# Attention units of four query blocks, with a unit's transpositions between the next unit's scores

## The chip, the cores and the metric

The kernel runs on one core of a Trainium2 chip. A core has engines that each run their own instructions in order and wait for one another by semaphores: TensorE (PE; its weight loads are shown as PEld), VectorE (DVE), ScalarE (ACT), GpSimd (POOL) and SyncE (SP), which issues the DMA transfers here. Matmuls write to PSUM; everything else lives in SBUF. The metric is the device time of one execution, in microseconds (us), as the median of several runs.

## The reference

A two-layer decoder trunk on one sequence of 1024 tokens of width 1024. Each layer projects the stream once and feeds four token mixers of four heads each (64 columns of values a head): MLA, stick-breaking attention, forgetting ("Fox") attention and cross-attention to a memory of 256 tokens. Three of them are causal: a block of 128 queries reads the keys up to its own end.

```python
def _layer(x, mem, cos, sin, w_in, ...):
    h = x @ w_in
    ...
    y_mla = _causal_softmax_attention(concat([q_nope, q_pe]), concat([k_nope, k_pe]), v_mla)
    y_sb = _stick_breaking_attention(sq, sk, sv)
    y_fox = _causal_softmax_attention(fq, fk, fv, log_decay=c)
    y_mem = _memory_attention(mem_q, mk, mv)
    ...
    for n in range(N_BRANCHES):
        yb = branches[n].reshape(b, s, BRANCH_WIDTH) * jax.nn.silu(gate_z[:, :, n])
        merged = merged + merge_g[:, :, n] * (yb @ w_branch[n])
    out = merged @ w_out
    return _layer_norm(DEEPNORM_ALPHA * x + out, ln_g, ln_b)
```

In a causal softmax mixer a query block does `logits = q k^T (+ decay)`, a row maximum, `exp`, a sum, and `p v`; stick-breaking has a suffix product over the keys of `1 - sigmoid` in place of the softmax. All is float32. The kernel writes most operands as a sum of two parts, a leading one (`h`) and the rest (`l`), and multiplies the parts apart.

## The kernel before

**Projections.** The projections keep 128 columns of weights on PE and move 512 tokens at a time: for each of eight contraction blocks three matmuls, `h h`, `l h`, `h l` (`passes`, L255 to L257). They are written as generators that stop after each such step, so that they can be handed out between the pieces of attention work: the *filler*.

**Units.** Attention is cut into units (`Unit`, L367): one head and one group `qg` of two query blocks, 256 queries. A unit has two parts:

- `scores` (L388): for each of its query blocks and each 512 keys a score tile `sc` in PSUM (two matmuls, L383 and L384, and a third for MLA, L386; the second uses `s2`, a copy of the queries with their two halves exchanged, which `swapped`, L360, makes with two DMAs). Fox and MLA: DVE adds bias or mask and takes the maximum (L441), ACT does `exp` (L135), DVE the reciprocal (L452), POOL the scaling (L453). Stick-breaking: ACT makes two sigmoids `kt` and `bt` of each tile (L135), DVE a scan (L446) and a product (L447).
- `values` (L463): PE transposes the probabilities by blocks of 128 x 128 (L472) into a PSUM tile `pt`: two key blocks x two query blocks, 512 columns, 384 on the diagonal. ACT copies it to `ph` (L155), DVE writes the rest `pl` (L156). `product` (L495), two `pt` later (`LAG`), multiplies: for each key block `y += v ph` and `y += v pl`, 256 columns each, 128 where the diagonal leaves one query block (L502). At a unit's end `add_heads` adds the two halves of `y` with ACT (`yc`, L490) and DVE (L491).

**Order.** `run` (L540) takes a list of units, writes a unit's scores, and then the values of the unit that lies two back (`AHEAD`). At each stop `gap` hands out so many steps of filler that `total` steps are spread evenly over all gaps of the run. The groups of a head come in the order 3, 0, 2, 1. A layer has six such runs: two Fox pairs (49 filler steps each), two stick-breaking pairs (65 and 64), memory (72) and MLA (54 steps of the merge between them, then `finish`). In the merge (`merge`, L1080) the gated branch outputs are split by `split_y` (ACT `ybh`, L158; DVE `ybl`, L159) from `y`, which `load_y` (L1062) reads back from a DRAM buffer `y_d`. The program is then put in order for each engine by a list scheduler of the framework, by its own durations; so the rows of an engine are not simply those of the text.

**Buffers that tie engines together.** PSUM: score tiles and projections share four buffers (`pj`, `sc`) that are handed out in the program's order; `pt` (and the transpositions `vtp` of a new pair's values, L336) has two, `y` has two.

## Time and profile before

| | |
|---|---|
| time, median of 3 runs | 1570.71 us (1570.52 to 1572.05) |
| the profiled execution | 1573.47 us, its span 1571.7 us |
| granted TensorE clock | 0.999 |
| PE matmuls of attention values (L502) | 1088: 896 of 256 columns, 192 of 128 |
| transpositions (L472) | 992, in 272 evacuations |

A row of the page's fifth part has line, engine, operation, `out<-in` with shapes and count, then busy time and the mean ns of one, then the idle time of that engine just before those rows and what ended it. A row of the timeline has start, duration, engine, line and operation, and in square brackets how long the engine had stood before it and for what. Matmuls overlap in the array, so the distance from one start to the next is what one costs, not the duration printed.

### The profile page before, as it was taken

Reading aid. Unit: us, or ns where it says so; the run is one execution under the profiler, and the core shown is the slowest. Engines: PE = TensorE matmul, PEld = TensorE weight load, DVE = VectorE, ACT = ScalarE, POOL = GpSimd, SP = SyncE. Lnnn points to the kernel's source line nnn. Section 1 sums busy time; section 2 is a strip of 40 time slices with the busy share of each in tenths; the row PEclk is TensorE's granted clock in tenths of the full one; section 3 lists DMA queues with packets and bytes.
Section 4 is the critical chain, followed back from the end, with each engine's and each line's share of the span. In section 5 each row is a group of like instructions: output and inputs, shape, how many; then the busy total and the mean of one; then the engine's idle time right before and its main releaser. Section 6 shows DMA issues by size and latency. Waiting matters only on the chain.

```text
span 1571.7 us, 24749 instructions
## 1 busy us (share of the span) xinstructions
PE 1552.4 (99%) x8446; PEld 1326.9 (84%) x8446; DVE 1034.5 (66%) x2055; ACT 726.9 (46%) x1608; POOL 781.1 (50%) x951
## 2 busy tenths in 40 slices
PE   9999999999999999999999999999999999999997
PEld 8888888888888788888898888888888888888886
DVE  7455687755436788882853566887554367898738
ACT  4355565545434666440323556655354346564400
POOL 5666536565544343671336655365565443436600
PEclk9999999999999999999999999999999999999999
DMA  6321112132233211252313211121322232212413
GB/s 185 113 73 42 46 47 70 58 100 76 76 107 110 68 45 55 80 175 74 124 55 106 60 47 48 42 75 51 108 70 80 102 111 71 65 41 78 154 53 115
DMA packets 86061, 127.92 MB, mean 81 GB/s; under 512 B 13424, under 2 KB 38832, under 8 KB 85936
## 3 DMA queue, kind: packets, MB, share of 16 engines
q1 hardware_dynamic: 85936, 126.34, 25.9%
q8 instruction: 67, 1.10, 0.3%
q14 instruction: 58, 0.48, 0.1%
HBM read 89.57 MB, written 19.96 MB: 70 GB/s over the span
## 4 chain that ended last, share of the span: by engine, by line
PE 92%; DVE 2%; POOL 2%; issue 2%; DMA 1%; ACT 1%; SPq 0%; DVEq 0%; POOLq 0%; ACTq 0%
PE pj L255 13%; PE pj L257 13%; PE pj L256 13%; PE y L502 7%; PE pt L472 6%; PE po L256 4%; PE po L257 4%; PE po L255 4%; PE sc L384 4%; PE sc L383 4%; PE pb L255 3%; PE pb L257 3%; PE pb L256 3%; PE pg L255 1%; PE pg L257 1%
## 5 line engine op out<-in xcount | busy, mean ns | idle before, releaser
L255 PE MATMUL pj<-xTh,wh 128*128 128x512 f32 x832 | 334.3, 402 | 2.3 <-DVE mx L441 1.4
L257 PE MATMUL pj<-xTh,wl 128*128 128x512 f32 x832 | 327.4, 393 | 0.0
L256 PE MATMUL pj<-xTl,wh 128*128 128x512 f32 x832 | 326.2, 392 | 0.0
L164 POOL TENSOR_SCALAR wh<-wr 128x512 fp32r<-128x512 f32 x168 | 114.9, 685 | 227.6 <-PE pj L256 147.1
L167 POOL TENSOR_TENSOR wl<-wr,wh 128x512 fp32r<-128x512 f32 x168 | 223.2, 1331 | 9.7
L156 DVE TENSOR_TENSOR pl<-pt,ph 128x384 fp32r<-128x384 f32 (+1 forms) x272 | 171.3, 639 | 85.0 <-ACT ph L155 83.2
L155 ACT CAST ph<-pt 128x384 fp32r<-128x384 f32 (+1 forms) x272 | 147.5, 549 | 151.3 <-PE pt L472 147.3
L257 PEld LDWEIGHTS pj<-xTh,wl 128*128 128x128 f32 x832 | 156.3, 188 | 31.6
L255 PEld LDWEIGHTS pj<-xTh,wh 128*128 128x128 f32 x832 | 156.7, 188 | 24.9 <-DVE mx L441 1.8
L256 PEld LDWEIGHTS pj<-xTl,wh 128*128 128x128 f32 x832 | 156.7, 188 | 22.5
L453 POOL TENSOR_SCALAR p<-p,sm 128x896 f32<-128x896 f32 (+7 forms) x128 | 102.7, 804 | 146.7 <-DVE sm L452 146.2
L135 ACT ACTIVATE p<-p,mx 128x896 f32<-128x896 f32 (+7 forms) x128 | 99.5, 777 | 68.0 <-DVE mx L441 61.0
L502 PE MATMUL y<-pl,v 128*128 128x256 f32 (+1 forms) x544 | 121.9, 301 | 0.0
L135 ACT ACTIVATE mg<-pg 128x512 f32<-128x512 f32 x128 | 76.1, 598 | 84.0 <-PE pg L257 43.1
L502 PE MATMUL y<-ph,v 128*128 128x256 f32 (+1 forms) x544 | 112.5, 282 | 2.1 <-ACT ph L155 1.9
L472 PE MATMUL pt<-ident_r,p 128*128 128x128 f32 x704 | 111.2, 273 | 0.3
L502 PEld LDWEIGHTS y<-ph,v 128*128 128x128 f32 x544 | 94.9, 189 | 16.3 <-ACT ph L155 2.1
L446 DVE TENSOR_TENSOR_SCAN kt<-kt,unseen 128x896 f32<-128x896 f32 (+3 forms) x64 | 95.2, 1490 | 19.8 <-ACT kt L135 19.3
L255 PE MATMUL pb<-ybh,wh 128*128 128x512 f32 x256 | 102.5, 400 | 1.5 <-ACT mg L135 0.7
L256 PE MATMUL pb<-ybl,wh 128*128 128x512 f32 x256 | 100.1, 391 | 0.0
L257 PE MATMUL pb<-ybh,wl 128*128 128x512 f32 x256 | 100.1, 391 | 0.0
L472 PEld LDWEIGHTS pt<-ident_r,p 128*128 128x128 f32 x704 | 85.1, 140 | 13.8 <-issue 0.5
(272 smaller groups left out, 3550.8 us busy)
## 6 DMA issues: line engine op xcount, KB each, us to landing
wr<-in_w_s_dram SPq DMA_DIRECT2D x168, 256.0 KB, 2.6
s<-opA SPq DMA_DIRECT2D x128, 64.0 KB, 2.0
s<-opB SPq DMA_DIRECT2D x128, 64.0 KB, 2.0
wr<-in_w_out_dram SPq DMA_DIRECT2D x32, 256.0 KB, 2.6
xr<-in_x_t_dram SPq DMA_DIRECT2D x16, 256.0 KB, 5.3
ckb<-c_d SPq DMA_DIRECT2D x8, 512.0 KB, 3.8
y_d<-y SPq DMA_DIRECT2D x16, 256.0 KB, 2.1
y<-y_d SPq DMA_DIRECT2D x16, 256.0 KB, 3.4
```

Source lines behind the costliest of these rows:

```text
L135: i = act.activation(*args, **kw)
L155: act.copy(h, src)
L156: return dve.tensor_tensor(l, src, f(h), ALU.subtract)
L164: i = pool.tensor_scalar(h, src, 1.0, 1.0, ALU.mult, ALU.mult)
L167: pool.tensor_tensor(l, src, f(h), ALU.subtract)
L255: pe.matmul(ps, ah, bh, start=k == 0, stop=False)
L256: pe.matmul(ps, ah, bl, start=False, stop=False)
L257: pe.matmul(ps, al, bh, start=False, stop=k == nk - 1)
L446: dve.tensor_tensor_scan(kt[:, ::-1], kt[:, ::-1], unseen[:, S - w:][:, ::-1], 1.0, ALU.mult, ALU.max)
L453: pool.tensor_scalar(p, p, sm, 1.0, ALU.mult, ALU.mult)
L472: pe.transpose(pt[:, c:c + P], self.p[i][:, b * P:(b + 1) * P], ident)
L502: pe.matmul(u.y[:, q0 * P:256], u.op["v"][b][:, u.head, :], src[:, s * 256 + q0 * P:s * 256 + 256], start=j == 0 and n == 0, stop=j == n_c ...
```

## The change

A unit now has one head and one *half*: four query blocks, 512 queries, in the order 1, 0. Four effects follow.

1. `chunks` gives one key block at a time, with the first query block `q0` that may see it: a `pt` holds one key block x four query blocks, 512 columns, and 384, 256 and 128 on the diagonal. `product` has two matmuls for it, `v ph` and `v pl`. Value matmuls, each with its weight load, fall from 1088 to 640; the columns that they move stay the same. The evacuations of `pt` rise from 272 to 320, some of them now 256 and 128 wide.
2. `s2` is 512 wide, with half as many DMAs of twice the size. `add_heads` works on 512 columns, half as often.
3. `run` no longer keeps two units in flight. While it writes a unit's scores, it takes the steps of the one unit before it between them, from the second score tile on, spread evenly; what is left comes behind the scores.
4. In the MLA run 100 - 26 - 16 steps are spread instead of 96 - 26 - 16; `finish` sets `prep[0]` behind the last product, so that the gates `pg` of the merge then use the buffers of `y`; and the first merge calls `split_y` for the next branch at its end, each half two stops later, instead of within its last column block.

```diff
-    def swapped(q, head, qg):
-        s2 = tp.tile([P, 256], F32R, tag="s2", name=nm("s2"), bufs=3)
-        src = q[head][qg // 2][:, (qg % 2) * 256:(qg % 2) * 256 + 256]
+    def swapped(q, head, half):
+        s2 = U("s2")
+        src = q[head][half]
...
-            for i in range(2):
-                qb = 2 * self.qg + i
+            for i in range(4):
+                qb = 4 * self.half + i
...
-            g = self.qg
-            return [[(2 * j, 0, 0), (2 * j + 1, 1, 0)] for j in range(g)] + [[(2 * g, 1, 0), (2 * g + 1, 0, 1)]]
+                return [(0, 0), (1, 0)]
+            return [(b, max(0, b - 4 * self.half)) for b in range(4 * self.half + 4)]
...
-                for b, s, q0 in ch:
-                    for i in range(q0, 2):
-                        c = s * 256 + i * P
-                        lo = min(lo, c)
-                        pe.transpose(pt[:, c:c + P], self.p[i][:, b * P:(b + 1) * P], ident)
+                for i in range(q0, 4):
+                    pe.transpose(pt[:, i * P:(i + 1) * P], self.p[i][:, b * P:(b + 1) * P], ident)
...
-        seq = [(b, s, q0, ph) for b, s, q0 in ch] + [(b, s, q0, pl) for b, s, q0 in reversed(ch)]
-        for n, (b, s, q0, src) in enumerate(seq):
-            pe.matmul(u.y[:, q0 * P:256], u.op["v"][b][:, u.head, :], src[:, s * 256 + q0 * P:s * 256 + 256],
-                      start=j == 0 and n == 0, stop=j == n_ch - 1 and n == len(seq) - 1)
+        for n, src in enumerate((ph, pl)):
+            pe.matmul(u.y[:, q0 * P:], u.op["v"][b][:, u.head, :], src[:, q0 * P:],
+                      start=j == 0 and n == 0, stop=j == n_ch - 1 and n == 1)
...
-            for _ in u.scores():
+            back = flight.pop(0) if flight else None
+            vals = back.values() if back else iter(())
+            n_vals = 2 * len(back.chunks()) if back else 0
+            told = 0
+            for n, _ in enumerate(u.scores(), 1):
+                gap()
+
+                while told * (u.n_scores - 1) < n_vals * max(0, n - 2):
+                    told += 1
+                    if next(vals, 0) == 0:
+                        break
+                    gap()
+            for _ in vals:
                 gap()
             flight.append(u)
-            if len(flight) > AHEAD:
-                for _ in flight.pop(0).values():
-                    gap()
...
-                    if ct == KT - 1 and following is not None:
+                    if ct == KT - 1 and following is not None and not first:
                         split_y(following, half)
...
+            if first:
+
+                for half in range(2):
+                    yield
+                    yield
+                    split_y(following, half)
...
-        run(units(ml[0], "mla") + units(ml[1], "mla"), mg, 96 - MG_EARLY - MG_LATE, False)
-        finish(mg, 1)
+        run(units(ml[0], "mla") + units(ml[1], "mla"), mg, 100 - MG_EARLY - MG_LATE, False)
+        finish(mg, 1, lambda: prep.__setitem__(0, True))
```

The mem units get two score tiles in the same way. Lines move by a few: the value matmuls are L495, the transpositions L467, `ph` and `pl` L153 and L154, the projections L253 to L255, the scores L382 and L383, the `v` copies L338 and L340, `add_heads` L484 and L485.

How the rows of an engine stand is shown at three places. The names are those of the tiles, with a number that tells one buffer's use from another.

The first place is the end of the first Fox pair and the start of the second (some 122 us into the program): PE's rows in the kernel before, where `pj` is the second pair's projection, `vtp` the transposition of its values, `sc` its first scores, and `pt` and `y` belong to the first pair's last units.

```order
L257 MATMUL pj_1634<-xTh_179,wl_1449 128x512
L336 MATMUL vtp_1589<-ident_r,vT_1576 128x128 x4
L383 MATMUL sc_1649<-opA_1321,opA_1182 128x512
L384 MATMUL sc_1649<-opA_1321,s_335_1600 128x512
L383 MATMUL sc_1656<-opA_1440,opA_1182 128x512
L384 MATMUL sc_1656<-opA_1440,s_335_1600 128x512
L472 MATMUL pt_1666<-ident_r,p_1359 128x128
L472 MATMUL pt_1666<-ident_r,p_1383 128x128
L472 MATMUL pt_1666<-ident_r,p_1359 128x128
L472 MATMUL pt_1666<-ident_r,p_1383 128x128
L255 MATMUL pj_1634<-xTh_187,wh_1454 128x512
L256 MATMUL pj_1634<-xTl_188,wh_1454 128x512
```

PE's rows of the changed kernel at the same place, from the last product of the last but one unit on (`y_1458`; the last projection matmul stands 13 rows ahead of it, and the next one 32 rows behind it, with values, `vtp` and scores alone between them):

```order
L495 MATMUL y_1458<-pl_1541,v_875 128x128
L467 MATMUL pt_1652<-ident_r,p_1348 128x128
L467 MATMUL pt_1652<-ident_r,p_1365 128x128
L467 MATMUL pt_1652<-ident_r,p_1379 128x128
L467 MATMUL pt_1652<-ident_r,p_1465 128x128
L467 MATMUL pt_1673<-ident_r,p_1365 128x128
L467 MATMUL pt_1673<-ident_r,p_1379 128x128
L467 MATMUL pt_1673<-ident_r,p_1465 128x128
L383 MATMUL sc_1612<-opA_1296,s_342_1597 128x512
L383 MATMUL sc_1616<-opA_1424,s_342_1597 128x128
L383 MATMUL sc_1646<-opA_1296,s_342_1597 128x512
L495 MATMUL y_1737<-ph_1657,v_863 128x512
```

Before, projections stand between the value copies, the scores and the products; now that stretch has none, and value matmuls, transpositions and scores follow one another.

ACT's rows for the same stretch of the changed kernel, in the order in which ACT takes them; `yc` is `add_heads`, `opA` and `opB` are the evacuations of the projection `pj`:

```order
L153 CAST ph_1540<-pt_1538 128x128
L338 CAST v_1580<-vtp_1575 128x4x64
L338 CAST v_1581<-vtp_1575 128x4x64
L338 CAST v_1591<-vtp_1586 128x4x64
L338 CAST v_1592<-vtp_1586 128x4x64
L484 COPY yc_1700<-y_1458 64x512
L306 ACTIVATE opA_1744<-pj_1631 64x512
L153 CAST ph_1657<-pt_1652 128x512
L153 CAST ph_1677<-pt_1673 128x384
L306 ACTIVATE opB_1745<-pj_1631 64x512
```

ACT's rows of the kernel before around the same second half of the `v` copies:

```order
L340 CAST v_1584<-vtp_1578 128x4x64
L135 ACTIVATE p_1608,sm_1610<-p_1608,mx_1609 128x896
L490 COPY yc_1679<-y_1474 64x256
L340 CAST v_1594<-vtp_1589 128x4x64
L340 CAST v_1595<-vtp_1589 128x4x64
L155 CAST ph_1671<-pt_1666 128x512
L490 COPY yc_1702<-y_1697 64x256
L135 ACTIVATE p_1642,sm_1644<-p_1642,mx_1643 128x1024
L135 ACTIVATE p_1727,sm_1729<-p_1727,mx_1728 128x128
```

The four `v` copies, which came in two pairs with other work between, now stand together, with `yc` and `opA` behind them, ahead of the first `ph` of the last unit.

The second place is the end of the last stick-breaking pair (some 295 us): DVE's rows with the longest scan in the kernel before, where `kt` is scanned, `bt` multiplied, and `pl` is an evacuation that a value matmul waits for.

```order
L447 TENSOR_TENSOR bt_3627<-bt_3627,kt_3628 128x895
L446 SCALAR_TENSOR_TENSOR kt_3668<-kt_3668,unseen 128x1024
L491 TENSOR_TENSOR y_3704<-y_3551,yc_3705 64x256
L156 TENSOR_TENSOR pl_3717<-pt_3711,ph_3716 128x512
L447 TENSOR_TENSOR bt_3667<-bt_3667,kt_3668 128x1023
```

One `pl` follows the scan, behind an addition of `y`. DVE's rows of the changed kernel at that place (`t` is a rotation's part):

```order
L927 TENSOR_TENSOR t_1210_5139<-rot_631,t_1210_5139 128x8x64
L446 SCALAR_TENSOR_TENSOR kt_3653<-kt_3653,unseen 128x1024
L154 TENSOR_TENSOR pl_3575<-pt_3569,ph_3574 128x512
L154 TENSOR_TENSOR pl_3599<-pt_3594,ph_3598 128x384
L447 TENSOR_TENSOR bt_3652<-bt_3652,kt_3653 128x1023
```

The scan stands ahead of evacuations in both; in the changed kernel two of them follow it at once, of a unit whose products come next on PE.

The third place is the start of the first Fox run (some 68 us): PE's rows in the kernel before, from the second to the third unit's scores (`sc`).

```order
L472 MATMUL pt_1040<-ident_r,p_888 128x128
L383 MATMUL sc_990<-opA_755,opA_712 128x512
L384 MATMUL sc_990<-opA_755,s_177_946 128x512
L383 MATMUL sc_997<-opA_786,opA_712 128x128
L384 MATMUL sc_997<-opA_786,s_177_946 128x128
L383 MATMUL sc_1014<-opA_755,opA_712 128x512
L384 MATMUL sc_1014<-opA_755,s_177_946 128x512
L383 MATMUL sc_1018<-opA_786,opA_712 128x256
L384 MATMUL sc_1018<-opA_786,s_177_946 128x256
L255 MATMUL pj_1055<-xTh_396,wh_794 128x512
L256 MATMUL pj_1055<-xTl_397,wh_794 128x512
```

Four score tiles are followed by a projection. PE's rows of the changed kernel, in the first unit's scores:

```order
L383 MATMUL sc_929<-opA_755,s_157_880 128x512
L382 MATMUL sc_936<-opA_786,opA_712 128x256
L383 MATMUL sc_936<-opA_786,s_157_880 128x256
L382 MATMUL sc_950<-opA_755,opA_712 128x512
L383 MATMUL sc_950<-opA_755,s_157_880 128x512
L382 MATMUL sc_957<-opA_786,opA_712 128x384
L383 MATMUL sc_957<-opA_786,s_157_880 128x384
L382 MATMUL sc_974<-opA_755,opA_712 128x512
L383 MATMUL sc_974<-opA_755,s_157_880 128x512
L382 MATMUL sc_978<-opA_786,opA_712 128x512
L383 MATMUL sc_978<-opA_786,s_157_880 128x512
L382 MATMUL sc_1000<-opA_755,opA_681 128x128
```

Where the tiles of two query blocks stood ahead of a projection, now those of four stand there, 640 to 1024 keys each, and the next unit's behind them.

More of the change, by code (lines that the diff above doesn't have):

```diff
@@ L24 @@
 DEPTH = 2
-AHEAD = 2
 LAG = 2
@@ L33 @@
 MG_LATE = 16
-Q_ORDER = (3, 0, 2, 1)
 NB = S // P
@@ L367, in decoder_trunk, with __init__ @@
     class Unit:
-        def __init__(self, op, head, qg, kind, aux=None):
-            self.op, self.head, self.qg, self.kind, self.aux = op, head, qg, kind, aux
+        def __init__(self, op, head, half, kind, aux=None):
+            self.op, self.head, self.half, self.kind, self.aux = op, head, half, kind, aux
             self.p = []
+            self.n_scores = 2 if kind == "mem" else 4 + 4 * half
         def prep(self):
-            self.s2 = swapped(self.op["q"], self.head, self.qg)
+            self.s2 = swapped(self.op["q"], self.head, self.half)
             if self.kind == "fox":
@@ L379, in qk @@
         def qk(self, o, i, kk, c0, n):
-            op, h, qg = self.op, self.head, self.qg
-            c = (qg % 2) * 256 + i * P
+            op, h, half = self.op, self.head, self.half
+            c = slice(i * P, (i + 1) * P)
             mla = self.kind == "mla"
-            pe.matmul(o, op["q"][h][qg // 2][:, c:c + P], kk, start=True, stop=False)
-            pe.matmul(o, self.s2[:, i * P:(i + 1) * P], kk, start=False, stop=not mla)
+            pe.matmul(o, op["q"][h][half][:, c], kk, start=True, stop=False)
+            pe.matmul(o, self.s2[:, c], kk, start=False, stop=not mla)
             if mla:
-                pe.matmul(o, op["qpe"][h][qg // 2][:, c:c + P], op["kpe"][c0 // HALF][:, :n], start=False, stop=True)
+                pe.matmul(o, op["qpe"][h][half][:, c], op["kpe"][c0 // HALF][:, :n], start=False, stop=True)
         def scores(self):
@@ L414, in scores @@
                 else:
-                    p = (K if i and self.kind == "mla" else W)("p", w)
+                    p = (K if i % 2 and self.kind == "mla" else W)("p", w)
                     bias = None
@@ L528, in decoder_trunk, with finish @@
     flight = []
-    def finish(filler, every):
+    def finish(filler, every, over=lambda: None):
         while flight:
@@ L537, in finish @@
             steps(filler, every)
+        over()
         drain(filler)
@@ L543, in run @@
         order = list(units)
-        gaps = sum(len(u.chunks()) * 2 + (1 if u.kind == "mem" else 2 + 2 * (u.qg // 2)) for u in units)
+        gaps = sum(len(u.chunks()) * 2 + u.n_scores for u in units)
         done = [0, 0]
@@ L742, in aux @@
                     return cell[0], c_nat, 2 * pair + h
-                us += [Unit(op, h, g, "fox", aux) for g in Q_ORDER]
+                us += [Unit(op, h, g, "fox", aux) for g in (1, 0)]
             return us
@@ L749, in units @@
         def units(op, kind):
-            return [Unit(op, h, g, kind) for h in range(2) for g in Q_ORDER]
+            return [Unit(op, h, g, kind) for h in range(2) for g in (1, 0)]
         ys = {}
```

58 lines of the change are left out of this document (28 added, 30 removed).

## The prediction

> **What bounds the kernel now.** I read the page's first part, then the chain of work that ended last, then PE's waits, and only then the timeline around the attention units.
>
> ```profile
> span 1571.7 us, 24749 instructions
> PE 1552.4 (99%) x8446; PEld 1326.9 (84%) x8446; DVE 1034.5 (66%) x2055; ACT 726.9 (46%) x1608; POOL 781.1 (50%) x951
> PE 92%; DVE 2%; POOL 2%; issue 2%; DMA 1%; ACT 1%; SPq 0%; DVEq 0%; POOLq 0%; ACTq 0%
> PE y L502 <- ACT ph L155: 1.9, 1, 1.9
> PE pj L255 <- DVE mx L441: 1.4, 2, 0.7
> PE sc L383 <- DVE acc L1104: 1.0, 2, 0.7
> ```
>
> TensorE is busy for 99% of the span and is 92% of the chain that ended last. The three longest rows of PE's waits inside the layers (us in total, times, longest) are small: PE hardly ever stands. So the change has two prices that count: the time that PE's own instructions take, and any time in which PE stands because ACT or DVE is late. An engine with 66% or 46% has room on average; whether it is late is a question of each place.
>
> **PE's own work.** PE matmuls go from 8426 to 7978: 800 fewer of 256 columns and 96 fewer of 128, 352 more of 512 and 96 more of 384. The printed durations (about 0.40 us) overlap, so the price is the distance from start to start.
>
> ```profile
> 115.37 0.39 PE L255 MATMUL pj<-xTh,wh 128*128 128x512 f32 x1
> ...
> 118.09 0.39 PE L255 MATMUL pj<-xTh,wh 128*128 128x512 f32 x1
> ```
>
> ```profile
> 301.57 0.40 PE L502 MATMUL y<-ph,v 128*128 128x256 f32 x2
> 301.80 0.39 PE L502 MATMUL y<-pl,v 128*128 128x256 f32 x2
> 302.03 0.39 PE L255 MATMUL pj<-xTh,wh 128*128 128x512 f32 x1
> ```
>
> ```profile
> 114.55 0.34 PE L383 MATMUL sc<-opB,opB 128*128 128x384 f32 x1
> 114.72 0.34 PE L384 MATMUL sc<-opB,s 128*128 128x384 f32 x1
> 114.90 0.40 PE L383 MATMUL sc<-opB,opB 128*128 128x512 f32 x1
> ```
>
> ```profile
> 122.35 0.60 PE L336 MATMUL vtp<-ident_r,vT 128*128 128x128 f32 x4
> 122.71 0.48 PE L383 MATMUL sc<-opA,opA 128*128 128x512 f32 x1
> 123.03 0.40 PE L384 MATMUL sc<-opA,s 128*128 128x512 f32 x1
> ```
>
> Between the two quoted L255 rows lie twelve starts in 2.72 us: 0.227 us for 512 columns. Four of 256 columns take 301.57 to 302.03, 0.115 each; the median over the trace is 0.118. One of 384 takes 0.175, the median is 0.173. Four of 128 and one of 512 take 122.35 to 123.03, 0.68, so one of 128 takes 0.11. A pair of 256 (0.236) thus costs nearly what one of 512 does. The sum: -800 x 0.118 - 96 x 0.109 + 352 x 0.227 + 96 x 0.173 = **-8.4 us**. With 256 columns at exactly half of 512 it would be -4.8; I take -8.4. Transpositions stay at 992.
>
> Two 256s cost that little only because their weight loads are hidden. In the trace every 512 has a load of its own, and still starts 0.227 after the last:
>
> ```profile
> L502 PEld LDWEIGHTS y<-ph,v 128*128 128x128 f32 x544 | 94.9, 189 | 16.3 <-ACT ph L155 2.1
> ```
>
> The Trainium skill, "TensorE: Matmul & The Clock Gate", Part 3, "The mechanism", says under what overlaps that a weight load overlaps matmuls in flight only when its row group differs. By that rule full-height loads would stand between the matmuls; the trace disagrees, since 0.189 of load and a 512's streaming do not fit one after the other into 0.227. What it would give is the third rival.
>
> **A wait that goes.** The first merge reads `y` back through DRAM, and ACT's in-order `ybh` holds up the evacuation behind it:
>
> ```profile
> 540.45 0.63 ACT L158 ACTIVATE ybh<-y 128x512 fp32r<-128x512 f32 x1 [3.42 <-DMA y<-y_d]
> 540.99 0.57 ACT L155 CAST ph<-pt 128x512 fp32r<-128x512 f32 x1
> 541.61 0.30 PEld L502 LDWEIGHTS y<-ph,v 128*128 128x128 f32 x2 [2.14 <-ACT ph L155]
> 542.46 0.19 PEld L383 LDWEIGHTS sc<-opA,opA 128*128 128x128 f32 x1 [0.55 <-DVE acc L1104]
> 1323.95 0.50 PE L383 MATMUL sc<-opA,opA 128*128 128x512 f32 x1 [0.69 <-DVE acc L1104]
> ```
>
> Here 2.1 + 0.5 in layer 0 and about 0.8 in layer 1 (0.7 on the row), 3.5 us together. `load_y` keeps its place in the merge, and `split_y` now comes up to four of the merge's steps later, so the read is back when ACT reaches it: **-3.5 us**, bounds -3.5 and 0 (if it is merely moved). Nothing else is late at that place but what the next part counts.
>
> **Waits that come.** Before, a unit's values stood between projections, so the evacuation of a `pt` (ACT `ph`, then DVE `pl`) had time: by the order of PE's rows the shortest cover of a `ph` was 1.5 us and one in ten had under 3.6. After, the shortest is 0.66 and one in ten has under 0.90; the time from one use of a `pt` buffer to the next falls from 1.9 to 0.9 at the shortest. What is needed:
>
> ```profile
> 302.73 0.60 PE L472 MATMUL pt<-ident_r,bt 128*128 128x128 f32 x4
> 303.36 0.59 ACT L155 CAST ph<-pt 128x512 fp32r<-128x512 f32 x1 [0.94 <-PE pt L472]
> ```
>
> ```profile
> L155 ACT CAST ph<-pt 128x512 fp32r<-128x512 f32 x176 | 102.8, 587 | 99.8 <-PE pt L472 96.2 <-PE y L502 2.0 <-ACT p L135 0.3
> L155 ACT CAST ph<-pt 128x384 fp32r<-128x384 f32 x96 | 46.2, 481 | 51.5 <-PE pt L472 51.1
> L340 ACT CAST v<-vtp 128x256 fp32r<-128x256 f32 x32 | 10.4, 378 | 8.2 <-PE vtp L336 4.4 <-issue 3.5
> L308 ACT ACTIVATE opA<-pj 64x512 fp32r<-64x512 f32 x56 | 33.0, 590 | 44.9 <-PE pj L257 40.9 <-DMA ckb<-c_d 3.4
> L135 ACT ACTIVATE kt<-sc 128x512 f32<-128x512 f32 x48 | 28.8, 601 | 10.5 <-PE sc L384 10.4
> L135 ACT ACTIVATE kt<-sc 128x128 f32<-128x128 f32 x16 | 4.6, 284 | 3.4 <-PE sc L384 3.2
> L156 DVE TENSOR_TENSOR pl<-pt,ph 128x512 fp32r<-128x512 f32 x176 | 120.6, 686 | 62.5 <-ACT ph L155 61.5
> L156 DVE TENSOR_TENSOR pl<-pt,ph 128x384 fp32r<-128x384 f32 x96 | 52.9, 551 | 22.5 <-ACT ph L155 21.8
> L312 DVE SCALAR_TENSOR_TENSOR opA<-pj,opA 64x512 fp32r<-64x512 f32 x56 | 38.3, 684 | 44.8 <-ACT opA L308 25.9 <-ACT opB L308 12.3 <-PE pj L257 5.5
> L441 DVE CUSTOM_DVE_ANT_0 p<-sc,p 128x512 f32<-128x512 f32 x40 | 27.4, 686 | 31.5 <-PE sc L384 21.4 <-POOL p L421 9.2 <-POOL p L453 0.6
> L342 DVE TENSOR_TENSOR v<-vtp,v 128x256 fp32r<-128x256 f32 x32 | 12.0, 418 | 1.6 <-ACT v L340 1.5
> L446 DVE TENSOR_TENSOR_SCAN kt<-kt,unseen 128x1024 f32<-128x1024 f32 x8 | 18.5, 2312 | 0.4 <-ACT kt L135 0.4
> ```
>
> ACT begins 0.3 us after the start of the last of four transpositions (0.33 into 302.73, then 303.36). A full `pt` is thus usable 0.3 + 0.587 = 0.9 us after it on `ph`, and 0.9 + 0.686 = 1.6 on `pl`. With ACT and DVE free that is covered nearly everywhere; with a queue in front of it, not. Four places, each once per layer:
>
> (a) *First Fox pair into the second* (the stretch shown with the change). Count from the end of the first `vtp` tile. ACT has, in order, four `v` (4 x 0.378), `yc` (512 wide and not in the trace; 0.59 like `opA`), `opA` 0.59, `ph` 0.587: ready at 0.3 + 3.28 + 0.05 = 3.6. PE has before that `ph`'s product two value matmuls, four transpositions, one value matmul, seven transpositions and three score matmuls: 2.1. It stands **1.5**. DVE, from the end of `yc` at 2.4: `y` 0.68, `opA` 0.684, `pl` 0.686, ready at 4.5; PE is there at 4.1: **0.4**. DVE's next row frees a score tile (0.686 and a 0.08 read) at 5.8, PE needs it at 5.4: **0.4**. Then `opB`, a `pl` of 256 (0.42, like `v`) and a row of 128 (half of a 512's 0.686, an estimate) free the next at 7.2, PE needs it at 6.1: **1.1**. Sum 3.4. Who else is late meanwhile: the softmaxes queued on ACT and DVE behind these; their `p` is wanted a unit later.
>
> (b) *Fox into stick-breaking.* From the first `vtp` tile the same chain: 1.5 for `ph` and 0.4 for `pl`. Behind `opB`, done at 4.6, ACT has the sigmoid pairs that free the score tiles: of 512 columns (2 x 0.60) until 5.8, where PE wants the tile at 5.4: 0.4; of 128 (2 x 0.28) until 6.4, wanted at 6.1: 0.3; of 512 until 7.6, wanted at 7.2 by the next projection: 0.4. Ahead of the chain lie the last half-1 values with no projection between: three times a `pt` buffer is wanted again before its `pl` (1.6 after its transpositions) is done, 0.2, 0.6 and 0.3. Sum 4.1.
>
> (c) *The last stick-breaking units.* A scan of 2.31 stands in DVE's queue ahead of a `pl` of 0.69, which is ready 3.05 after the scan begins. Beside the scan ACT has the last sigmoid and the `ph` (0.60 + 0.587), so PE passes that `ph`'s product at about 1.25 and comes to the transposition that needs the `pt` buffer at 1.5: it stands 1.5, and 0.5 for the `ph` behind the sigmoids before. Sum 2.0.
>
> (d) *The first Fox scores*: score tiles wait for DVE already:
>
> ```profile
> 76.25 0.19 PEld L383 LDWEIGHTS sc<-opA,opA 128*128 128x128 f32 x1 [0.45 <-DVE mx L441]
> 77.43 0.19 PEld L255 LDWEIGHTS pj<-xTh,wh 128*128 128x128 f32 x1 [0.88 <-DVE mx L441]
> ```
>
> These two made about 1.0 of standing (0.2 and 0.8 over the pace). Now four rows of 640 to 1024 keys stand there, where there were two, and the four score tiles in PSUM come free in DVE's order. From the end of the first score tile: its row 0.3 + 0.686 + 0.08 frees a tile at 1.1, PE wants it at 0.3: 0.7. `opA` and a row of 128 free the next at 2.2, wanted at 1.3: 0.9. A row of 512 and `opB` (0.76 + 0.69) free the third at 3.7, wanted at 2.7: 1.0. The later three come by the same steps to 0.2, 0.3 and 0.6. Sum 3.7, +2.7 over before.
>
> Six smaller places (elsewhere in Fox and stick-breaking, the starts of memory and MLA, MLA's widest rows) come by the same steps to 3 to 6 us a layer; small waits are those a slightly early queue swallows, so I take 1.5. A layer: 3.4 + 4.1 + 2.0 + 2.7 + 1.5 = 13.7; two layers **+27.4**. Bounds: 3 a layer, if ACT and DVE are ahead at each of these places by one evacuation more than I worked out, and 19 with every place in full: +6 and +38. `s2` halves its number of transfers and is issued a whole unit ahead; I cost it at nothing, with a unit's scores and values (some 10 us) as its cover.
>
> **Sum.** -8.4 - 3.5 + 27.4 = +15.5 on the profiled execution of 1573.5 (span 1571.7), which is 2.8 above the median of 1570.7; so **1586.2** as a median. The bounds: 1570.7 - 11.9 + 6 = 1565 and 1570.7 - 11.9 + 38 = 1597, or 1600 with `y`'s wait merely moved.
>
> **The rivals.** *The covers hold (the other side).* The mechanism is PE's saving with ACT and DVE ahead of it everywhere: 46% and 66% busy speak for it, the queues of (a) to (c) against. Its price is 1570.7 - 11.9 + 2 to 8 = 1561 to 1567, and with no new wait 1558.8; it decides if the new waits come to under 4.4 us a layer. Chance 0.25. *It balances*: 4.4 to 7.5 us a layer, 1568 to 1574, chance 0.12. *Loads are not hidden*: 448 fewer value loads of 0.189 would bring -85 and some 1486; the 0.227 between two 512s speaks against it, and I give it 0.01. *Forecast*: waits over 7.5 a layer, 1574 to 1600, chance 0.62.
>
> **How the numbers follow.** Likeliest 1586. About 0.2% (3.1 us) is what a measurement of this kernel can tell from no change. Faster is the first and third rival, 0.26; same 0.12; slower 0.62. The range runs from 1562, inside the first rival, to 1600, the upper bound: it leaves out about 0.1 on each side. The forecast's own range is 1574 to 1600.
>
> **What would show it.** Right: PE's waits name `y` <- ACT `ph` or DVE `pl`, `pt` <- DVE `pl`, and score tiles <- DVE or ACT, in clumps near 75 to 80, 125 to 135, 180 to 200 and 300 to 310 us and again some 785 us later, each 2 to 4 us long; the wait at 541 is gone; DVE and ACT keep their shares. Wrong: if those stretches show PE starts at the pace of 0.227 with no standing, the chain of (a) is false, and the time lies near 1560. If the waits are there but the time is below 1574, the sizes are; if PE's sum of paces has not fallen by about 8, the first term is.

## The result, and the profile after

The changed kernel takes **1621.59 us** (median of 4 runs, 1620.42 to 1624.44) against 1571.38 us for the kernel before in the same comparison (4 runs): a ratio of 1.0324, 95% interval 1.0312 to 1.0337. It is slower, as forecast, but by 50 us where 15 were forecast, and outside the range of 1562 to 1600.

Three lines of the page of the changed kernel, the span, the busy times and the chain that ended last:

```profile
span 1619.8 us, 23500 instructions
...
PE 1567.1 (97%) x7998; PEld 1307.3 (81%) x7998; DVE 1038.1 (64%) x2039; ACT 719.4 (44%) x1592; POOL 793.1 (49%) x951
...
PE 83%; DVE 8%; issue 4%; POOL 2%; ACT 1%; DMA 1%; SPq 0%; DVEq 0%; POOLq 0%; ACTq 0%
```

PE has 448 matmuls fewer, no engine is busy for a larger share of the span, and the span is 48 us longer: PE's share of the last chain falls from 92% to 83%, and DVE's rises from 2% to 8%. PE is not the only one on the path any more. PE's waits of the changed kernel (us in total, times, longest), the larger ones:

```profile
PE pt L467 <- DVE pl L154: 10.4, 12, 3.1
PE sc L382 <- DVE mx L441: 5.3, 9, 0.8
PE sc L382 <- DVE opB L310: 4.4, 5, 1.9
PE pj L253 <- ACT bt L133: 3.6, 2, 1.8
PE pb L253 <- DVE mgl L154: 3.4, 2, 1.7
PE mk L253 <- ACT p L133: 3.0, 2, 1.5
PE pt L467 <- DVE bt L447: 2.4, 2, 1.2
...
PE sc L383 <- DMA s<-opA: 1.4, 1, 1.4
```

All rows of that view come to 42 us, where before they came to 10. A finer measure is the distance from each PE start to the next, less the pace of that width (0.227 us for 512 columns, and so on, as in the prediction). Delays of over 0.15 us each come to 14.9 us before and 63.9 after: **+49.0 us**. That is as much as the whole loss; what is left of the span, 1571.7 - 14.9 = 1556.8 and 1619.8 - 63.9 = 1555.9, hardly differs. Most of these delays are waits, in clumps, where one engine's queue was in the way of another's; a part is not waiting, but matmuls that ran at half the clock (last section). One clump in the timeline of the changed kernel, of PE, ACT and DVE in the last stick-breaking units:

```profile
322.44 0.51 PE L467 MATMUL pt<-ident_r,bt 128*128 128x128 f32 x3
322.46 1.00 ACT L153 CAST ph<-pt 128x512 fp32r<-128x512 f32 x2
322.58 3.36 DVE L446 TENSOR_TENSOR_SCAN kt<-kt,unseen 128x1024 f32<-128x1024 f32 x1
...
323.14 0.45 PE L495 MATMUL y<-ph,v 128*128 128x512 f32 x1
...
325.86 1.12 DVE L154 TENSOR_TENSOR pl<-pt,ph 128x512 fp32r<-128x512 f32 x2
326.67 0.41 PE L467 MATMUL pt<-ident_r,bt 128*128 128x128 f32 x2 [3.08 <-DVE pl L154]
```

This is place (c) of the prediction as it was described, only longer: PE wants a `pt` buffer whose `pl` stands behind a scan, and stands for 3.1 us.

The wait on `ybh` that the kernel before had at 541 us is gone: no row of L156, which is `ybh`'s line now, waits for a DMA any more.

### The profile page after: what moved, and what is told of

Its sections match the earlier page's. It is cut to its first block, busy times and chain, and to the rows that moved or that the text cites. A ratio compares the mean times of both kernels' runs of the same rounds, so it can differ in the third digit from the quotient of the medians.

```text
span 1619.8 us, 23500 instructions
## 1 busy us (share of the span) xinstructions
PE 1567.1 (97%) x7998; PEld 1307.3 (81%) x7998; DVE 1038.1 (64%) x2039; ACT 719.4 (44%) x1592; POOL 793.1 (49%) x951
## 4 chain that ended last, share of the span: by engine, by line
PE 83%; DVE 8%; issue 4%; POOL 2%; ACT 1%; DMA 1%; SPq 0%; DVEq 0%; POOLq 0%; ACTq 0%
PE pj L253 11%; PE pj L254 11%; PE pj L255 11%; PE y L495 6%; PE pt L467 6%; PE po L255 4%; PE po L254 4%; PE po L253 4%; PE sc L382 3%; PE pb L253 3%; PE pb L255 3%; PE pb L254 3%; PE sc L383 3%; PE pg L253 2%; PE pg L254 1%
## 5 line engine op out<-in xcount | busy, mean ns | idle before, releaser
L253 PE MATMUL pj<-xTh,wh 128*128 128x512 f32 x832 | 331.7, 399 | 3.9 <-ACT bt L133 3.6
L255 PE MATMUL pj<-xTh,wl 128*128 128x512 f32 x832 | 327.7, 394 | 0.0
L154 DVE TENSOR_TENSOR pl<-pt,ph 128x512 fp32r<-128x512 f32 (+1 forms) x320 | 173.6, 564 | 136.8 <-ACT ph L153 135.8
L165 POOL TENSOR_TENSOR wl<-wr,wh 128x512 fp32r<-128x512 f32 x168 | 242.7, 1446 | 10.2
L153 ACT CAST ph<-pt 128x512 fp32r<-128x512 f32 (+1 forms) x320 | 152.2, 493 | 210.8 <-PE pt L467 205.8
L453 POOL TENSOR_SCALAR p<-p,sm 128x640 f32<-128x640 f32 (+7 forms) x128 | 101.4, 795 | 184.7 <-DVE sm L452 181.6
L253 PEld LDWEIGHTS pj<-xTh,wh 128*128 128x128 f32 x832 | 157.0, 189 | 36.9 <-ACT bt L133 4.7
L255 PEld LDWEIGHTS pj<-xTh,wl 128*128 128x128 f32 x832 | 157.2, 189 | 33.1
L495 PE MATMUL y<-pl,v 128*128 128x512 f32 (+1 forms) x320 | 129.9, 407 | 0.0
L133 ACT ACTIVATE p<-p,mx 128x640 f32<-128x640 f32 (+7 forms) x128 | 99.2, 776 | 66.0 <-DVE mx L441 56.7
L467 PE MATMUL pt<-ident_r,p 128*128 128x128 f32 x704 | 119.5, 275 | 8.4 <-DVE pl L154 4.3
L467 PEld LDWEIGHTS pt<-ident_r,p 128*128 128x128 f32 x704 | 86.5, 140 | 35.6 <-DVE pl L154 9.9
L495 PE MATMUL y<-ph,v 128*128 128x512 f32 (+1 forms) x320 | 114.2, 357 | 0.2
L253 PE MATMUL pb<-ybh,wh 128*128 128x512 f32 x256 | 101.1, 395 | 3.7 <-DVE mgl L154 3.4
L255 PE MATMUL pb<-ybh,wl 128*128 128x512 f32 x256 | 100.0, 391 | 0.0
L433 POOL TENSOR_SCALAR_AFFINE_SELECT bt<-bt 128x128 f32<-128x128 f32 x64 | 48.1, 757 | 104.3 <-ACT bt L133 104.3
L446 DVE TENSOR_TENSOR_SCAN kt<-kt,unseen 128x640 f32<-128x640 f32 (+3 forms) x64 | 95.8, 1511 | 4.2 <-ACT kt L133 4.0
```

The lines of the kernel that those rows point to most:

```text
L133: i = act.activation(*args, **kw)
L153: act.copy(h, src)
L154: return dve.tensor_tensor(l, src, f(h), ALU.subtract)
L165: pool.tensor_tensor(l, src, f(h), ALU.subtract)
L253: pe.matmul(ps, ah, bh, start=k == 0, stop=False)
L255: pe.matmul(ps, al, bh, start=False, stop=k == nk - 1)
```

## The experiments

The theories at the start: **O**, the order (a unit's values beside the next unit's scores, only one unit in flight) takes the projections' cover away; **W**, the width of the units does. Times are medians; each is compared with runs of the kernel before on the same chip (1571 to 1572 us). `...` in an edit stands for lines left out.

**1. Weaving alone, on the old units.** `before` with the changed kernel's `run`:

```diff
-            for _ in u.scores():
+            back = flight.pop(0) if flight else None
+            vals = back.values() if back else iter(())
...
+            for _ in vals:
                 gap()
             flight.append(u)
-            if len(flight) > AHEAD:
-                for _ in flight.pop(0).values():
-                    gap()
```

> Units of two query blocks as before, but with the changed run: one unit in flight, its transpositions and products between the next unit's score tiles. PE's work is that of before. Theory O (the lost time comes from the order: a unit's values stand right behind its scores and beside the next scores, where the projections covered them): 1595 to 1620 us, with PE waits on pt <- DVE pl and sc <- DVE of 25 us and more. Theory W (it comes from the width: eight score tiles in a row against four PSUM buffers, and evacuations of 512 columns one behind the other): 1568 to 1580, PE waits below 15 us.

Measured 1567.47 us, ratio 0.9974 (0.9962 to 0.9986): slightly *faster* than before, by 0.3%, and just under the range of theory W. Delays over 0.15 us fell from 14.9 to 10.0 us.

**2. The new units without weaving.** `after` with a unit's values behind all of the next unit's scores:

```diff
-            for n, _ in enumerate(u.scores(), 1):
-                gap()
...
-            for _ in vals:
+            for _ in u.scores():
                 gap()
             flight.append(u)
+            if len(flight) > 1:
+                for _ in flight.pop(0).values():
+                    gap()
```

> Units of four query blocks as in the changed kernel, but nothing woven: a unit's values come behind all of the next unit's scores, as before with two. Theory O: the projections cover both again, 1560 to 1575 us. Theory W: 1605 to 1625, with the waits on score tiles (sc <- DVE mx, opB; pj <- ACT bt) kept or larger, since eight score tiles still come in a row; the waits pt <- DVE pl would then be fewer than the 10.4 us of the changed kernel.

Measured 1613.63 us, 1.0266 (1.0245 to 1.0286). Most of the loss stays, as theory W has it; against its expectation the waits of `pt` for `pl` are longer (14.8 us in sum), not fewer. It is still 8 us less than the changed kernel's 1621.59, so on the new units the weaving itself costs some 8 of the 50 us.

**3. One unit ahead, on the old units.**

```diff
-AHEAD = 2
+AHEAD = 1
```

> The kernel before with one unit ahead in place of two (AHEAD = 1), nothing woven, two query blocks. It tells apart the two halves of theory O. If the distance counts (a unit's probabilities are wanted sooner): 1585 to 1610 us, with PE waits pt <- POOL p, pt <- DVE bt. If only the weaving counts, or the width: 1569 to 1576.

Measured 1565.90 us, 0.9964 (0.9949 to 0.9979). That is below both expectations. Delays over 0.15 us fell to 8.2 us. Theory O falls as the main cause with these three: on the old units neither the weaving nor the distance costs anything, both gain, and on the new units the weaving costs a sixth of the loss.

**4. The merge's part alone.** `before` with 100 steps, `split_y` at the first merge's end, and `pg` in the buffers of `y` at the end:

```diff
-                    if ct == KT - 1 and following is not None:
+                    if ct == KT - 1 and following is not None and not first:
                         split_y(following, half)
...
-        run(units(ml[0], "mla") + units(ml[1], "mla"), mg, 96 - MG_EARLY - MG_LATE, False)
-        finish(mg, 1)
+        run(units(ml[0], "mla") + units(ml[1], "mla"), mg, 100 - MG_EARLY - MG_LATE, False)
+        finish(mg, 1, lambda: prep.__setitem__(0, True))
```

> The kernel before with the change's part in the MLA run alone (100 steps, split_y behind the first merge's end, the gates pg in the buffers of y at the end). My term: the waits of 2.6 and 0.8 us behind ybh go, -3.5 us: 1567 us. If the wait is only moved: 1570 to 1572. If the 100 steps take cover from the last MLA units: up to 1575.

Measured 1568.56 us, 0.9981 (0.9971 to 0.9990): -2.9 us for my term of -3.5.

**5. s2 in buffers of its own, on the new units.** The change had also moved `s2` from a ring of three into the pool of 64 that nearly everything shares.

```diff
-        s2 = U("s2")
+        s2 = tp.tile([P, HALF], F32R, tag="s2", name=nm("s2"), bufs=3)
-    up = ctx.enter_context(tc.tile_pool(name="up", bufs=64))
+    up = ctx.enter_context(tc.tile_pool(name="up", bufs=62))
```

> The changed kernel with the exchanged queries s2 in three buffers of their own, as before, in place of the pool of 64 that everything else uses (that pool has 62). If the late s2 transfers at the start of a run (a wait on DMA s of 1.4 us was seen) are what pushes scores back and leaves the rest in clumps: 1575 to 1605. If not: 1615 to 1625.

Measured 1601.48 us, 1.0188 (1.0168 to 1.0209): 20 us of the 50.

**6. The new units with the old packing of the values** (two key blocks x two query blocks in a `pt`, products of 256 columns; `s2` still in the pool):

```diff
-            return [(b, max(0, b - 4 * self.half)) for b in range(4 * self.half + 4)]
+            for s in range(2):
+                g = 2 * self.half + s
+                out += [(s, [(2 * j, 0, 0), (2 * j + 1, 1, 0)]) for j in range(g)]
+                out += [(s, [(2 * g, 1, 0), (2 * g + 1, 0, 1)])]
+            return out
...
```

`values` and `product` follow these chunks, and the memory units are packed in the same way.

> Units of four query blocks with eight score tiles, s2 and weaving as in the changed kernel, but the values packed as before: two key blocks x two query blocks in one pt, products of 256 and 128 columns, first the lower two query blocks and then the upper two, into one y of 512. PE's work is that of before again (+8). Theory B (the burst of scores of a wide unit, against four PSUM buffers shared with the projections): 1610 to 1635, the waits stay. Theory P (the packing: a pt needs the rows of four query blocks, and the diagonal leaves small pt that ask for a buffer more often): 1568 to 1590.

Measured 1596.48 us, 1.0157 (1.0136 to 1.0177), outside both expectations: 25 us of the 50 go although PE has 8 us more to do, and half stays. So the packing is a cause, and not the only one.

**7. The halves in the order 0, 1.**

```diff
-                us += [Unit(op, h, g, "fox", aux) for g in (1, 0)]
+                us += [Unit(op, h, g, "fox", aux) for g in (0, 1)]
...
-            return [Unit(op, h, g, kind) for h in range(2) for g in (1, 0)]
+            return [Unit(op, h, g, kind) for h in range(2) for g in (0, 1)]
```

> The changed kernel with a head's halves in the order 0, 1. A run then begins with a unit of four small score tiles and ends with the unit of eight key blocks. If the waits belong to the starts of runs because a long unit's first probabilities are late: 1590 to 1605. If they belong to any wide unit with no projection beside it: 1615 to 1630, the clumps only elsewhere.

Measured 1586.38 us, 1.0092 (1.0072 to 1.0113): 35 us of the 50 go, more than was expected. Inside a run the units and what they are woven with are nearly the same; it is the ends and starts of runs that differ. I take it from this that most of the loss sits there; the run doesn't show it place by place.

**8. Both of 5 and 7.**

```diff
-    up = ctx.enter_context(tc.tile_pool(name="up", bufs=64))
+    up = ctx.enter_context(tc.tile_pool(name="up", bufs=62))
...
-        s2 = U("s2")
+        s2 = tp.tile([P, HALF], F32R, tag="s2", name=nm("s2"), bufs=3)
...
-                us += [Unit(op, h, g, "fox", aux) for g in (1, 0)]
+                us += [Unit(op, h, g, "fox", aux) for g in (0, 1)]
...
```

> The changed kernel with both single edits that helped: s2 in three buffers of its own (-20 us alone) and a head's halves in the order 0, 1 (-35 us alone). If they act on different waits: 1565 to 1570. If both act on the same starts of runs: 1580 to 1586.

Measured 1580.67 us, 1.0058 (1.0035 to 1.0081). They act in great part on the same places: 41 us together, not 55.

**9. The two gains on the old units together** (3 and 4).

```diff
-AHEAD = 2
+AHEAD = 1
...
-                    if ct == KT - 1 and following is not None:
+                    if ct == KT - 1 and following is not None and not first:
...
```

> The kernel before with one unit ahead (-5.5 us measured) and the change's part in the MLA run (-2.9 us measured). If the two take away different waits: 1563 us. If both take away the same wait behind ybh: 1565 to 1567.

Measured 1563.71 us, 0.9947 (0.9930 to 0.9964): the best version found, 8 us under the kernel before. The two take away different waits.

**10. s2 in the pool, on the old units.** The woven kernel of experiment 1 with one line changed:

```diff
-        s2 = tp.tile([P, 256], F32R, tag="s2", name=nm("s2"), bufs=3)
+        s2 = U("s2")[:, :256]
```

> The narrow woven kernel (1567.5 us) with one edit: s2 comes from the pool of 64 in place of three buffers of its own, as in the changed kernel. In the program that puts the first Fox transfers of s2 behind three loads of projection weights in SP's queue. Theory R (the place of s2 alone makes scores late at the starts of runs): 1580 to 1590, PE waits in clumps near 74, 135 and 200 us and a wait on DMA s. Theory B (late s2 only costs where eight score tiles follow): 1567 to 1572.

Measured 1599.20 us, 1.0179 (1.0149 to 1.0208): **+31.7 us from this line**, on units that have nothing else of the change but the weaving, and more than either theory allowed. What the line does is to be seen in SP's queue. The timeline of SP in the kernel before, where the first Fox units' `s2` goes out ahead of three loads of weights:

```profile
45.46 0.52 SPq L364 DMA_DIRECT2D s<-opA  x1
...
46.66 0.50 SPq L363 DMA_DIRECT2D s<-opA  x1
...
57.20 14.28 SPq L231 DMA_DIRECT2D wr<-in_w_s_dram  x3
```

and in the changed kernel, where the first `s2` comes behind that weight load:

```profile
56.65 13.44 SPq L229 DMA_DIRECT2D wr<-in_w_s_dram  x3
70.14 0.52 SPq L361 DMA_DIRECT2D s<-opA  x1
70.71 0.58 SPq L362 DMA_DIRECT2D s<-opA  x1
```

They are 25 us later, and PE, which reaches the second score matmul of that unit, stands for the transfer (a row of PE's weight loads, changed kernel):

```profile
73.98 0.53 PEld L383 LDWEIGHTS sc<-opA,s 128*128 128x128 f32 x3 [1.84 <-DMA s<-opA]
```

Counted over PE's matmuls, that one is now the 385th of the program in place of the 355th, with projections and transpositions moved ahead of it. In the kernel of experiment 10 it is the 385th too, and its first `s2` goes out at 69.24 us; yet none of PE's waits there is for `s2`. So it is not the wait for the transfer that costs the 31.7 us. My reading, from the order and the traces, which no run shows by itself: the list scheduler, by whose own durations the transfer is late, puts projections ahead of the scores, and when the scores' turn comes there is no projection left to put between them: scores, value copies, transpositions and products come as one clump, and then ACT's and DVE's queues set the pace. That is the stretch without projections that the part on the change shows.

**11. A smaller pool.** `s2` in its own ring, the pool cut from 64 to 61 (woven, old units):

```diff
-    up = ctx.enter_context(tc.tile_pool(name="up", bufs=64))
+    up = ctx.enter_context(tc.tile_pool(name="up", bufs=61))
```

> The narrow woven kernel (1567.5 us), s2 in its own three buffers, the common pool cut from 64 to 61. If it is the fullness of the pool that costs (s2 just takes two or three buffers more of it): 1585 to 1600, like s2 in the pool (1599.2). If it is which buffer s2 gets (one that the pair's last projection frees only just ahead of the run): 1567 to 1569.

Measured 1564.81 us, 0.9961 (0.9941 to 0.9980). Three buffers fewer in the pool are not the cause; the kernel is even a little faster than either expectation.

**12. s2 in the pool, its transfers on ACT's queue** (experiment 10 with two more lines):

```diff
-        nc.sync.dma_start(f(s2[0:64, :]), f(src[64:128, :]))
-        nc.sync.dma_start(f(s2[64:128, :]), f(src[0:64, :]))
+        nc.scalar.dma_start(f(s2[0:64, :]), f(src[64:128, :]))
+        nc.scalar.dma_start(f(s2[64:128, :]), f(src[0:64, :]))
```

> The narrow kernel with s2 in the pool of 64 (1599.2 us), its transfers issued from ACT's queue in place of SP's, so that no load of weights stands ahead of them. If SP's queue (12.5 us in which a weight load waits for POOL) is what makes s2 late: 1568 to 1578. If it is the buffer, and with it the place of the second score matmul in PE's order: 1595 to 1602.

Measured 1613.84 us, 1.0268 (1.0239 to 1.0298): worse than on SP's queue, and outside both expectations. PE now waits for `s2` too, 10 us in all. The timeline of ACT and its queue in this kernel:

```profile
71.32 0.37 ACT L340 CAST v<-vtp 128x256 fp32r<-128x256 f32 x1 [4.27 <-PE vtp L336]
71.33 0.51 ACTq L363 DMA_DIRECT2D s<-opA  x1
...
71.93 0.55 ACTq L364 DMA_DIRECT2D s<-opA  x1
```

No weight load stands ahead of it now, and `s2` still goes out only at 71.33 us. But ACT's copy of the pair's last values stands ahead of it here, which waited 4.27 us for their transposition, so this run only moved `s2` behind something else. It shows that taking the weight loads out of its way is not enough. My guess is the buffer: if a tile of the pool gets one that was given up shortly before, then ahead of a run that is one of the pair's own projection. I did not give `s2` an old buffer of the pool, so that stays open; shown is what the line costs, on old units and new.

**13. s2 in its own ring, old packing, new units** (5 and 6 together):

```diff
-    up = ctx.enter_context(tc.tile_pool(name="up", bufs=64))
+    up = ctx.enter_context(tc.tile_pool(name="up", bufs=62))
...
-        s2 = U("s2")
+        s2 = tp.tile([P, HALF], F32R, tag="s2", name=nm("s2"), bufs=3)
...
-            return [(b, max(0, b - 4 * self.half)) for b in range(4 * self.half + 4)]
+            for s in range(2):
+                g = 2 * self.half + s
+                out += [(s, [(2 * j, 0, 0), (2 * j + 1, 1, 0)]) for j in range(g)]
+                out += [(s, [(2 * g, 1, 0), (2 * g + 1, 0, 1)])]
+            return out
...
```

> Units of four query blocks with s2 in its own three buffers (1601.5 us) and the values packed as before (two key blocks x two query blocks, 8.4 us more of PE's work). Of the 34 us that this width still costs over the narrow units: if they come from the packing and the small diagonal tiles (pt <- DVE pl, 12.2 us of waits): 1570 to 1582. If from the burst of eight score tiles: 1600 to 1612.

Measured 1571.60 us, 1.0001 (0.9990 to 1.0012). With both gone the wide units cost 4 us against experiment 1 and nothing against the kernel before: the burst of eight score tiles is all but harmless.

**14. The new packing below the diagonal only.** One key block x four query blocks where all four see it, two x two on the diagonal, `s2` in its own ring and the pool of 62, as in 5:

```diff
...
-            return [(b, max(0, b - 4 * self.half)) for b in range(4 * self.half + 4)]
+            d = 4 * self.half
+            out = [((b, 0, 4, 0),) for b in range(d)]
+            for r in range(2):
+                out += [((d + 2 * j, 2 * r, 2 * r + 2, 0), (d + 2 * j + 1, 2 * r, 2 * r + 2, 256)) for j in range(r)]
+                out += [((d + 2 * r, 2 * r, 2 * r + 2, 256), (d + 2 * r + 1, 2 * r + 1, 2 * r + 2, 128))]
+            return out
...
```

> Units of four query blocks with s2 in its own three buffers, key blocks below the diagonal packed as in the changed kernel (one key block x four query blocks, 512 wide), the diagonal part as before (two key blocks x two query blocks). It lies between wide_s2ring (1601.5 us, all of it packed by key block) and wide_nv_s2ring (1571.6 us, nothing). If the small diagonal tiles (384, 256, 128 wide, each with its own buffer of pt) cost the 30 us: 1568 to 1577. If it is that a pt needs the rows of all four query blocks: 1585 to 1600.

Measured 1582.00 us, 1.0067 (1.0044 to 1.0090), between the two expectations: of the 30 us between 1601.5 and 1571.6 some 20 go with the small diagonal tiles, some 10 stay with the wide ones.

The woven runs with the halves in the order 1, 0 in one table, with PE's own work by the paces and the delays over 0.15 us:

| units, packing | s2 | time | PE's work | delays |
|---|---|---|---|---|
| two blocks, old | own ring | 1567.5 | 1531.6 | 10.0 |
| two blocks, old | pool | 1599.2 | 1531.6 | 39.9 |
| four blocks, old | own ring | 1571.6 | 1531.6 | 12.8 |
| four blocks, old | pool | 1596.5 | 1531.6 | 36.2 |
| four blocks, diagonal old | own ring | 1582.0 | 1529.3 | 25.0 |
| four blocks, by key block | own ring | 1601.5 | 1523.2 | 47.8 |
| four blocks, by key block (the change) | pool | 1621.6 | 1523.2 | 63.9 |

Down a column of the table: the pool costs 20 to 32 us on any unit, the packing 25 to 30 in spite of 8 us less work, the width of the unit alone 4 and -3.

## Why the prediction was wrong, point by point

**The direction and the kind of loss were right.** PE's waits are on `pl`, on score tiles and on a sigmoid, in clumps near the places named, twice per kernel, and the other engines nearly keep their shares. The time came out slower because waits outgrew a small saving, as forecast; their size was not.

**"-8.4 us" of PE's own work.** By the widths the paces add up as said (1531.6 to 1523.2). But the rest of the span, without the long delays, fell by only 0.9 us. With `s2` in its own ring it fell by 5 (1599.5 - 47.8 = 1551.7). So the saving is partly eaten by delays below 0.15 us. By the starts of the matmuls, some 3.5 us of these lie in the half-clock stretches of the last section, where a matmul of 256 columns is late by about 0.1; the other 4 stay open. (The prediction's counts of matmuls, 8426 and 7978, are 20 below the page's 8446 and 7998; the difference is the same.)

**"-3.5 us" at `ybh`.** Confirmed by experiment 4 at -2.9, and by the row that is gone.

**The step that failed: "`s2` halves its number of transfers and is issued a whole unit ahead; I cost it at nothing".** It counted the transfers and the 10 us of cover, and not that the tile moved to another pool. The edit `s2 = U("s2")` stood in the diff. It is two fifths of the loss here (20 us of 50; 31.7 us on the old units), and without it place (a) looks otherwise. The same stretch with `s2` in its own ring, PE's timeline of experiment 5 behind the last `vtp`:

```profile
135.08 0.31 PE L495 MATMUL y<-pl,v 128*128 128x128 f32 x1
135.22 0.44 PE L253 MATMUL pj<-xTh,wh 128*128 128x512 f32 x1
135.51 0.39 PE L254 MATMUL pj<-xTl,wh 128*128 128x512 f32 x1
...
142.20 0.33 PE L383 MATMUL sc<-opA,s 128*128 128x384 f32 x1
142.37 0.40 PE L495 MATMUL y<-ph,v 128*128 128x512 f32 x1
```

Between the values of the last unit and the next product of a `ph` stand 24 projection matmuls at their pace, and the delays at 135 to 146 us shrink from 3.1 us in sum to a single one of 0.4. At (b) and (c) the ring alone doesn't help: 5.2 us of delays stand at 203 to 208 us, which is (b), and one of 4.1 at 319, which is (c).

**The mis-sized term: "six smaller places ... I take 1.5".** Delays over 0.15 us in layer 0 from 60 us on came to 7.6 us before and 32.1 after. By place, as growth over the kernel before:

| place | forecast | before | after | growth |
|---|---|---|---|---|
| (a) first Fox pair into the second, 135 to 146 us | 3.4 | 0 | 3.1 | 3.1 |
| (b) Fox into stick-breaking, 198 to 207 | 4.1 | 0 | 3.0 | 3.0 |
| (c) last stick-breaking units, 326 to 329 | 2.0 | 0 | 3.7 | 3.7 |
| (d) first Fox scores, 74 to 82 | 2.7 | 1.0 | 4.7 | 3.7 |
| `ybh` at 541 (a term of its own) | -2.6 | 2.6 | 0 | -2.6 |
| all others | 1.5 | 4.0 | 17.6 | 13.6 |

The four chains worked by hand come to 13.5 us against a forecast of 12.2, each within a factor of two. That the sum comes so near is partly luck: (b) was taken too long by 1.1 us and (c) too short by 1.7, of which 1.05 is a scan that took 3.36 us in place of 2.31. The places that I put into one term grew by nine times what I took, and by more than twice the 3 to 6 us that I had worked out for them: the first stick-breaking unit (4.9 at 213 to 231 us, the half clock of the last section in it, as in (d) and at the start of MLA), the first memory units (1.7 at 386), MLA's start (4.7 at 540 to 552) and its end (1.9 at 694). The first stick-breaking unit has the same kind of queue as (b). "Small waits are those a slightly early queue swallows" was an assumption that no row carried. Layer 1 grew by the same 25 us. This term and the one above overlap: with `s2` in its own ring the delays of layer 0 are 24.5 us in place of 32.1. What the growth is made of the table of runs shows: 25 to 30 us of the 50 go with the packing, by experiment 14 some 20 of them with the small diagonal tiles, and the prediction had no term for either. In its working, (a) adds 1.3 us between its `pl` and the freed score tile where its words account for 0.8, and the bound of 19 us a layer is 0.8 above its own places in full (12.2 and 6); neither changes the account.

**(a) was right for a partly wrong reason.** I took the missing projections as a given of the new units. They come with the place of `s2`: in its own ring, on the same units, the projections are there, as the rows above show.

**The rival "the covers hold"** needed under 4.4 us of new waits a layer; there were some 25. It is what happens on the old units: 1567.5 us for the weaving, where the projections do stay between.

**The weight loads.** The changed kernel has 448 loads fewer, and nothing of the 85 us that the third rival promised is to be seen; that rival is closed, as the pace of 0.227 us said.

## What to carry to other kernels

When an edit gives a tile another pool, price it as a change of its own, and compare the order of the rows around the tile's first use: here one such line cost 20 to 32 us, and in the order the second score matmul stood 30 matmuls later. A kernel whose bound engine is 99% busy has no slack to lend: look up, for *each* place where the covering work runs out, the longest in-order queue that then sets the pace, and do not lump the small ones. Fewer, wider instructions gained little here (8 us), as the narrow ones already ran at nearly the same pace per column, while the small tiles of the diagonal, each with a buffer of its own, cost some 20.

## What was not expected of the hardware

TensorE's granted clock fell to about half after clumps of waits. Busy times of PE, PEld, DVE, ACT and POOL in three stretches of the changed kernel, then PE's granted clock, DMA share and GB/s:

```profile
222.00:226.00 4.00, 2.19 (x11) 1.55 (x10) 3.58 (x6) 2.84 (x6) 0.84 (x1) 1.00 0.11 28
226.00:230.00 4.00, 4.00 (x12) 3.15 (x11) 3.88 (x6) 1.73 (x4) 1.36 (x2) 0.57 0.00 0
230.00:234.00 4.00, 4.00 (x23) 3.34 (x23) 2.77 (x3) 1.68 (x4) 3.66 (x4) 1.00 0.20 66
```

and the matmuls on the way into it:

```profile
224.68 0.50 PE L253 MATMUL pj<-xTh,wh 128*128 128x512 f32 x1 [1.81 <-ACT bt L133]
...
225.73 0.40 PE L254 MATMUL pj<-xTl,wh 128*128 128x512 f32 x1
225.96 0.45 PE L255 MATMUL pj<-xTh,wl 128*128 128x512 f32 x1
226.21 0.63 PE L253 MATMUL pj<-xTh,wh 128*128 128x512 f32 x1
226.64 0.63 PE L254 MATMUL pj<-xTl,wh 128*128 128x512 f32 x1
227.06 0.63 PE L255 MATMUL pj<-xTh,wl 128*128 128x512 f32 x1
```

From 226.2 us on a matmul of 512 columns starts 0.43 us after the last in place of 0.23, for 3.4 us, and PE does half as many in 4 us (12 against 23) with nothing to wait for. So 1.6 us were lost *after* a wait of 1.8 us. The mean clock was 0.991, and the trace's clock has seven such stretches of 3.41 us, 23.9 us in all, ahead of the one at the program's end, which the kernel before has too and which is its only one. At half the clock that is at most 12 us of the 50; by the starts of the matmuls in them I estimate 9. The runs differ in this as well: 27.3 us at half clock in experiments 5 and 10, 17.1 in 6, 3.4 in 13, none in 1 and 14. So a part of what the table puts down to the pool and to the packing is the clock. The same at (c) in experiment 5, where the half clock begins within a wait of 3.8 us, with the same columns:

```profile
314.00:318.00 4.00, 1.49 (x12) 1.17 (x10) 3.88 (x2) 3.55 (x9) 4.00 (x4) 1.00 0.00 0
...
321.70:325.00 3.30, 3.30 (x9) 2.62 (x9) 1.70 (x6) 0.20 (x1) 0.00 (x0) 0.50 0.00 0
325.00:328.00 3.00, 3.00 (x15) 2.43 (x15) 0.00 (x0) 0.00 (x0) 0.00 (x0) 1.00 0.00 0
```

The Trainium skill, "TensorE: Matmul & The Clock Gate", Part 1, says that the half clock comes after an idle window of about 3.4 us. Neither of the two places agrees to the letter: PE was busy for 2.19 of the 4 us ahead of the first and for 1.49 of those ahead of the second, and at (c) in the changed kernel a single wait of 3.1 us was followed by a full clock. What the traces show is a grid. The seven stretches begin at 75.96, 226.15, 386.57, 547.00, 1031.69, 1192.12 and 1352.55 us, and all distances between them are whole multiples of 3.413 us. Cut along that grid, the first place and (c) of the changed kernel look like this:

```profile
222.73:226.15 3.42, 1.61 (x8) 1.23 (x7) 3.00 (x6) 2.89 (x6) 0.84 (x1) 1.00 0.00 0
226.15:229.56 3.41, 3.41 (x9) 2.64 (x9) 3.32 (x5) 1.68 (x3) 0.92 (x2) 0.50 0.00 0
...
321.72:325.13 3.41, 1.87 (x15) 1.56 (x14) 3.41 (x2) 2.91 (x6) 3.33 (x3) 1.00 0.30 84
325.13:328.55 3.42, 1.85 (x10) 1.33 (x10) 3.42 (x5) 1.44 (x6) 1.36 (x3) 1.00 0.16 55
328.55:331.96 3.41, 3.41 (x15) 2.82 (x16) 3.32 (x9) 0.49 (x2) 0.20 (x1) 1.00 0.02 5
```

A window in which PE was busy for 47% was followed by a half-clock one; the wait of 3.1 us fell across two windows, each busy for 54 or 55%, and was not. In the whole changed kernel all five windows below 50% were followed by half clock, and two of the eight between 53 and 56%. So a wait of some 2 us can cost up to 1.7 us more behind it, by where it falls on the grid; the exact limit stays open, and the prediction had no term for it.

The scan of 1024 columns, 2.31 us on average in the kernel before, took 3.36 at the place shown above; why, no run here tells.
